# A diffusion block in fp32 on one core: the feed forwards as 2x2 block products with seven products for eight

## The chip, the cores and the metric

The kernel runs on one core of a Trainium2 chip. A core has five engines that work side by side, each through its own instructions in order: TensorE (PE; its weight loads are shown apart as PEld), VectorE (DVE), ScalarE (ACT), GpSimd (POOL) and SyncE (SP), which here starts nearly all DMAs. They share an SBUF of 128 partitions; matmuls are added up in PSUM. The metric is the time on the device of one execution, in microseconds (us), as the median of the runs.

## The reference

Two layers over 512 tokens `x` and 256 context tokens of 1024 values. Each layer is a feed forward, an attention (a grouped-query one with a window in layer 0, differential attention in layer 1) and a second feed forward; each is normed, scaled and shifted by a modulation, and its result is added to the residual:

```python
def _pre(h, gain, shift, scale):
    return _rmsnorm(h, gain) * (1.0 + scale) + shift

def _swiglu(h, w_gate, w_up, w_down):
    return (jax.nn.silu(h @ w_gate) * (h @ w_up)) @ w_down
...
        mx = (silu_c @ ada_w[i] + ada_b[i]).reshape(B, N_MOD, 1, D)
...
        fx = _swiglu(_pre(hx, norm_w[i, 0], mx[:, 0], mx[:, 1]), ffn_w_gate[i, 0], ffn_w_up[i, 0], ffn_w_down[i, 0])
        hx = hx + 0.5 * mx[:, 2] * fx
```

The context takes the same path with a modulation of its own; in the last feed forward (layer 1, the second) and in the final norm only `x` is left. Gate and up are 1024 x 2816, down 2816 x 1024; `ada_w` is 1024 x 9216 in each layer.

## The kernel before

All is held transposed: the residual `hT` is [128, 8, 768], eight blocks of 128 features for 768 tokens (256 of the context first). Every product takes three passes: each operand is split into a high part (rounded to float32r) and the rest, and high x high, high x low and low x high are added up in fp32 in PSUM. The gained residual stands split in `xh` and `xl`, with two more columns for the shift vectors. The norm's factor `rstd`, one per token, is applied after the product.

Weights are split when they are used. `weights` loads a packed 128 x 1024 unit (SP), casts it to the high part on ScalarE (L55) and subtracts that on GpSimd for the low part (L56); its pool holds two of each tile.

A block of gate or up (128 of 2816 columns, 22 blocks each) is `project`: 48 matmuls of 384 or 386 columns (L265) into two PSUM banks, then VectorE takes the bias columns (L270) and multiplies by `rstd` (L303). `up_block` runs it for gate and for up, then silu on ScalarE, (up + bias) x gate on VectorE (L952, the context's 256 columns and the 512 of `x`), the high part of the hidden block on ScalarE (L956) and its low part on GpSimd (L957).

Down follows in five groups of hidden blocks (`GROUPS`), each behind the first `up_block` of the next: for each of the eight output blocks a weight unit of 512 or 640 columns, `gemm` with the context's 256 and `x`'s 512 columns (L68, L70, L72), and `residual` on VectorE (L310). Behind the last group `after` makes squares and split parts of the block for what comes next. In the last feed forward all is done for the 512 columns of `x` alone (256 and 256), and `finish` takes the last group and the final norm, half of the tokens after the other.

The modulation is a matrix product with a vector, made on VectorE: `ada_block` loads 128 x 1024 of `ada_w` and multiplies with silu of the condition, with the sum as a second result (L130), once for `x` and, but for some of layer 1's, once for the context. The first 16 blocks come in `start` (twelve products there on GpSimd, L822), 56 in the first feed forward and 72 in the second, three and four behind each `up_block`.

The order on each engine is set when the program is built, by the framework's scheduler with its own model of times (`schedule_with_timeline_sim`); on the chip each queue runs in that order. L284, L491, L735 and others belong to the attentions.

## Time and profile before

| | |
|---|---|
| median of 3 runs | 2944.39 us (2941.35 to 2953.21) |
| profiled execution, first to last instruction | 2950.6 us |
| mean granted clock of TensorE | 0.977 |
| busy: PE, DVE, POOL, ACT | 95%, 53%, 44%, 33% |
| start and first feed forward | 0 to 656 us |
| window attention | to 1012 |
| second and third feed forward | to 1600 and 2155 |
| differential attention | to 2560 |
| last feed forward and final norm | to 2951 |

The profiled execution has no time but its span; it lies within the range of the timed runs. In rows that group instructions stand the line, the engine, the operation, what is written <- what is read by the program's names, the tile and how many; behind the bar the busy time, the mean of one in ns, and the engine's idle time ahead of them with what ended it. Rows by stretch give the busy time of each engine, the granted clock, the share of the DMA engines and GB/s. A timeline's row is start, duration, engine, line and operation.

### The profile page before, as it was taken

How to read it: one execution, taken by the hardware profiler on the slowest of the kernel's cores; microseconds unless marked ns; L12 is line 12 of the kernel's file. 1: busy time of each engine (PE TensorE's matmuls, PEld its weight loads, DVE VectorE, ACT ScalarE, POOL GpSimd, SP SyncE). 2: the span in 40 equal slices, each digit the busy share in tenths (PEclk: the TensorE clock that was granted, in tenths of full speed). 3: DMA queues.
4: the chain of work that ended last, by engine and by line, in shares of the span. 5: the costliest groups of instructions: out<-in, count | busy, mean ns of one | idle time of the engine just before them, and what ended most of it. 6: DMA issues, size and time to landing. Idle time of an engine off the chain costs nothing. (4 is left out here: it accounts for less than half of the span.)

```text
span 2950.6 us, 40979 instructions
## 1 busy us (share of the span) xinstructions
PE 2792.7 (95%) x16150; PEld 2608.6 (88%) x16150; DVE 1562.3 (53%) x2683; ACT 969.9 (33%) x1749; POOL 1303.5 (44%) x762
## 2 busy tenths in 40 slices
PE   5889999999989989999999999999999999999998
PEld 4878899999878888889999999999988888799998
DVE  7999422257787799632224322223267687522223
ACT  4211122144666421112223212122245565423223
POOL 5333333354543433333335333333365665656553
PEclk8999999999999999999999999999999999999999
DMA  6355212233342445631222121221122333233331
GB/s 236 123 175 201 86 58 72 65 102 102 84 140 76 139 158 192 236 94 54 68 65 65 59 63 58 71 63 50 61 85 79 88 88 105 93 93 102 101 100 64
DMA packets 113424, 296.38 MB, mean 100 GB/s; under 512 B 12880, under 2 KB 30928, under 8 KB 113232
## 3 DMA queue, kind: packets, MB, share of 16 engines
q1 hardware_dynamic: 112944, 293.66, 31.3%
q8 instruction: 128, 2.10, 0.3%
q14 instruction: 64, 0.52, 0.1%
q10 hardware_dynamic: 288, 0.10, 0.0%
HBM read 260.42 MB, written 15.20 MB: 93 GB/s over the span
## 5 line engine op out<-in xcount | busy, mean ns | idle before, releaser
L56 POOL TENSOR_TENSOR w_lo<-w_raw,w_hi 128x1024 fp32r<-128x1024 f32 (+2 forms) x377 | 793.2, 2105 | 1057.9 <-ACT w_hi L55 1037.0
L265 PE MATMUL big<-xh,w_hi 128*128 128x384 f32 (+3 forms) x2816 | 700.7, 330 | 44.0 <-DVE xh L830 16.3
L265 PE MATMUL big<-xh,w_lo 128*128 128x384 f32 (+3 forms) x2816 | 698.9, 330 | 21.4 <-POOL w_lo L56 21.4
L265 PE MATMUL big<-xl,w_hi 128*128 128x384 f32 (+3 forms) x2816 | 696.3, 328 | 4.3 <-DVE xl L831 4.3
L55 ACT CAST w_hi<-w_raw 128x1024 fp32r<-128x1024 f32 (+2 forms) x377 | 337.1, 894 | 1100.0 <-PE big L70 340.9
L265 PEld LDWEIGHTS big<-xh,w_hi 128*128 128x128 f32 x2816 | 505.4, 192 | 54.7 <-DVE xh L830 19.6
L265 PEld LDWEIGHTS big<-xh,w_lo 128*128 128x128 f32 x2816 | 501.8, 192 | 25.1 <-POOL w_lo L56 24.8
L265 PEld LDWEIGHTS big<-xl,w_hi 128*128 128x128 f32 x2816 | 504.0, 192 | 4.8 <-DVE xl L831 4.6
L270 DVE COPY bias<-big 128x2 f32<-128x2 f32 x176 | 27.7, 157 | 743.2 <-PE big L265 743.2
L130 DVE SCALAR_TENSOR_TENSOR ada_junk<-ada_raw,s_bc 128x1024 f32<-128x1024 f32 x224 | 339.7, 1549 | 44.8 <-DMA ada_raw<-ada_w 44.0
L310 DVE SCALAR_TENSOR_TENSOR hT<-big,mod,hT 128x512 f32<-128x512 f32 (+1 forms) x288 | 168.0, 619 | 352.7 <-PE big L72 352.6
L72 PE MATMUL big<-hh,w_lo 128*128 128x512 f32 (+1 forms) x1200 | 330.0, 347 | 7.7 <-POOL w_lo L56 7.7
L68 PE MATMUL big<-hh,w_hi 128*128 128x512 f32 (+1 forms) x1200 | 329.7, 346 | 0.7 <-ACT w_hi L55 0.7
L70 PE MATMUL big<-hl,w_hi 128*128 128x512 f32 (+1 forms) x1200 | 328.0, 344 | 0.0
L957 POOL TENSOR_TENSOR hl<-tb,hh 128x768 fp32r<-128x768 f32 (+1 forms) x88 | 153.1, 1740 | 262.5 <-ACT hh L956 239.7
L72 PEld LDWEIGHTS big<-hh,w_lo 128*128 128x128 f32 x1200 | 225.5, 189 | 38.5 <-POOL w_lo L56 10.0
L70 PEld LDWEIGHTS big<-hl,w_hi 128*128 128x128 f32 x1200 | 226.8, 189 | 30.6
L68 PEld LDWEIGHTS big<-hh,w_hi 128*128 128x128 f32 x1200 | 226.2, 189 | 29.5 <-ACT w_hi L55 1.4
L956 ACT CAST hh<-tb 128x768 fp32r<-128x768 f32 (+1 forms) x88 | 68.7, 781 | 347.6 <-DVE tb L952 347.6
L284 PE MATMUL half<-xh,w_hi 128*128 128x384 f32 (+3 forms) x464 | 156.1, 336 | 21.5 <-DVE ta L296 19.7
L952 DVE SCALAR_TENSOR_TENSOR tb<-tb,bias,ta 128x512 f32<-128x512 f32 (+1 forms) x154 | 169.2, 1132 | 6.8
L284 PE MATMUL half<-xl,w_hi 128*128 128x384 f32 (+3 forms) x464 | 154.2, 332 | 0.0
(215 smaller groups left out, 3689.8 us busy)
## 6 DMA issues: line engine op xcount, KB each, us to landing
w_raw<-ffn_gu SPq DMA_DIRECT2D x176, 512.0 KB, 3.3
ada_raw<-ada_w SPq DMA_DIRECT2D x144, 512.0 KB, 3.6
w_raw<-ffn_d SPq DMA_DIRECT2D x96, 256.0 KB, 2.7
w_raw<-ffn_d SPq DMA_DIRECT2D x64, 320.0 KB, 2.9
w_raw<-diff_in SPq DMA_DIRECT2D x24, 512.0 KB, 3.3
w_raw<-gqa_in SPq DMA_DIRECT2D x12, 512.0 KB, 3.4
og<-god SPq DMA_DIRECT2D x6, 768.0 KB, 5.9
w_raw<-gqa_out SPq DMA_DIRECT2D x8, 512.0 KB, 3.6
```

Of the source, the lines that this page charges most:

```text
L55: nc.scalar.copy(out=hi[:, :cols], in_=raw[:, :cols])
L56: nc.gpsimd.tensor_tensor(out=lo[:, :cols], in0=raw[:, :cols], in1=hi[:, :cols].bitcast(F32), op=ALU.subtract)
L68: nc.tensor.matmul(o, wh, xh, start=(k == 0), stop=False)
L70: nc.tensor.matmul(o, wh, xl, start=False, stop=False)
L72: nc.tensor.matmul(o, wl, xh, start=False, stop=(k == n - 1))
L130: getattr(nc, engines[s]).scalar_tensor_tensor(out=junk, in0=raw, scalar=1.0, in1=self.sbc[:, s], op0=ALU.mult, op1=ALU.mult, accum_out=se ...
L265: mm(ps[:, c, :e - s], w[:, k], x[:, k, s:e], start=first, stop=last)
L284: mm(ps[:, :e - s], w_[:, k], x[:, k, s:e], start=(k == 0 and i == 0), stop=(k == ND - 1 and i == 2))
L310: self.nc.vector.scalar_tensor_tensor(out=h, in0=o, scalar=self.mv(l, s, c, d), in1=h, op0=ALU.mult, op1=ALU.add)
L952: nc.vector.scalar_tensor_tensor(out=u[:, tk], in0=u[:, tk], scalar=bu[:, s:s + 1], in1=g[:, tk], op0=ALU.add, op1=ALU.mult)
L956: nc.scalar.copy(out=hh[:, toks], in_=u[:, toks])
L957: nc.gpsimd.tensor_tensor(out=hl[:, toks], in0=u[:, toks], in1=hh[:, toks].bitcast(F32), op=ALU.subtract)
```

## The change

The products of the feed forwards are written as 2x2 blocks. The left operand's four blocks are gate and up (or two output blocks of down) by the even and the odd 128-row blocks of the contracted side; the right operand's are the even and odd blocks by two halves of the tokens (384 and 384, in the last feed forward 256 and 256; the two bias columns go with the first half). Instead of eight block products there are seven of sums and differences (the Winograd form): `a_operands` loads four raw tiles of 512 columns for one block of gate and of up, makes four sums on VectorE (L116) and splits seven operands, the high parts on ScalarE and the low ones on GpSimd (L112). Raw tiles and sums come from one pool of eight buffers (`sf`), split operands from a ring of eight. `b_combine` makes the seven right operands (four differences on VectorE, L150; splits on GpSimd, L146 and L172, one on VectorE), once per feed forward for the input (`x_pair`) and once for the hidden blocks (`h_pair`).

The seven products go to three PSUM banks, with 84 matmuls for 96 per block of gate and up. The sums behind them are copies on ScalarE and additions from PSUM on VectorE (L1107, L1111, L1116, L1079); gate and the second half of up are multiplied by `rstd` on GpSimd (L1112, L1117). Product 4 of a block follows in the next. All blocks of gate and up come first; the hidden blocks are written to DRAM (`hs`) and read back in pairs for down, which has four groups (`PAIRS`, two pairs of hidden blocks and three times three) of four pairs of output blocks, with the additions straight into `hT` (L1139). In down an operand has 256 or 384 columns.

`next_pair` makes the next feed forward's operands behind each output pair; the squares' sums all move to VectorE (L245). The modulation blocks are spread over three feed forwards (48, 32, 48; L317), at most three behind a block of gate and up. In `start` only products 1, 5 and 2 of the first block are begun (before: three blocks). `finish` isn't split in halves. The attentions read the same split parts from other tiles, and their weights are split in tiles of 512.

```diff
-GROUPS = (5, 5, 4, 4, 4)
+KP = ND // 2
+PAIRS = (2, 3, 3, 3)
...
+    def sf_open(self, side="right"):
+        self.sf = self.sb("sums", 8, side=side)
...
+    PROD = {1: (0, 0), 2: (1, 1), 3: (6, 2), 4: (2, 6), 5: (4, 3), 6: (5, 4), 7: (3, 5)}
...
+    def a_operands(self, src, n):
...
+        def load(*bs):
+            for b in bs:
+                raws[b] = self.sf.tile([P, 512], F32, name="sf")[:, :n * P]
+                nc.sync.dma_start(raws[b], src[:, b])
+        def split(b, f):
+            ts[b] = self.wtile()
+            hi, lo = (ts[b][:, p, :n * P] for p in range(2))
+            nc.scalar.copy(out=hi, in_=f)
+            eng = nc.vector if b in self.dve_a else nc.gpsimd
+            eng.tensor_tensor(out=lo, in0=f, in1=hi.bitcast(F32), op=ALU.subtract)
...
+        def total(x, y, op=ALU.subtract):
+            t = self.sf.tile([P, 512], F32, name="sf")[:, :n * P]
+            nc.vector.tensor_tensor(out=t, in0=x, in1=y, op=op)
+            return t
...
+        load(0, 3, 2)
+        s1 = total(raw(3), raw(2), ALU.add)
+        s3 = total(raw(0), raw(3))
+        s2 = total(s1, raw(0))
+        split(0, raw(0))
+        split(4, s1)
+        load(1)
+        s4 = total(raw(1), s2)
+        split(1, raw(1))
+        split(5, s2)
+        split(6, s4)
+        split(3, s3)
+        split(2, raw(2))
...
+    def b_combine(self, t, w, f, splits):
...
+        t1 = diff(f(5), f(0))
+        if splits:
+            split(0, f(0))
+        split(3, t1)
+        if splits:
+            split(1, f(1))
+        t3 = diff(f(2), f(5))
+        t2 = diff(f(2), t1)
+        split(5, t3)
+        if splits:
+            split(2, f(2))
+        else:
+            raw = t[:, 0:3, 1, :w].bitcast(F32)
+            hi = t[:, 0:3, 0, :w]
+            nc.scalar.copy(out=hi, in_=raw)
+        t4 = diff(f(1), t2)
+        split(4, t2)
+        split(6, t4)
+        if not splits:
+            nc.gpsimd.tensor_tensor(out=t[:, 0:3, 1, :w], in0=raw, in1=hi.bitcast(F32), op=ALU.subtract)
+    def product(self, p, bank, aops, bops, w, ks=None, first=False):
...
+        wh, wl = aops[self.PROD[p][0]]
+        n = len(wh)
+        slot = self.PROD[p][1]
+        for k in (range(n) if ks is None else ks):
...
+            for x, y, go, end in ((wh[k], xh, first and k == 0, False), (wh[k], xl, False, False),
+                                  (wl[k], xh, False, k == n - 1)):
+                mm(bank[:, :w], x, y, start=go, stop=end, skip_group_check=not first)
...
+        parts = ((0, 2 * j, 0), (5, 2 * j, 1), (1, 2 * j + 1, 0), (2, 2 * j + 1, 1))
+        self.b_combine(t, B + m, source, True)
...
+    def squares(self, d, xonly=False):
...
+                sq = self.sf.tile([P, 512], F32, name="sf")[:, :m]
+                nc.scalar.activation(out=sq, in_=h[:, tk], func=AF.Square)
+                nc.vector.tensor_tensor(out=self.acc[:, tk], in0=sq, in1=self.acc[:, tk], op=ALU.add)
...
+    def next_pair(self, pools, l, n, j, xonly=False):
...
+        for d in (2 * j, 2 * j + 1):
+            self.squares(d, xonly)
+        t = self.optile(pools[0] if j < 3 else pools[1], xonly)
+        self.x_pair(t, l, n, j, xonly)
+        self.x.append(t)
...
+            if d % 2:
+                t = self.optile(pools[0] if d < 6 else pools[1], False)
+                self.x_pair(t, 0, 0, d // 2, False)
+                self.x.append(t)
+                self.up_begin(first, (d // 2,))
...
-        self.ffn(0, 0, False, [(0, b) for b in range(16, 72)], to_gqa, True)
...
-        self.ffn(0, 1, False, [(1, b) for b in range(72)],
-                 lambda d: (self.x_bias(1, 0) if d == 0 else None, self.x_block(1, 0, d)))
...
-        self.ffn(1, 0, False, [], lambda d: (self.x_bias(1, 1) if d == 0 else None, self.x_block(1, 1, d)))
...
+        self.ffn(0, 0, False, (self.opx, self.opy), [(0, b) for b in range(16, 64)], to_attention(0), True)
+        self.gqa()
+        pools = (self.opy, self.opx)
+        self.ffn(0, 1, False, pools, [(0, b) for b in range(64, 72)] + [(1, b) for b in range(24)],
+                 lambda j: self.next_pair(pools[::-1], 1, 0, j))
+        self.ffn(1, 0, False, pools[::-1], [(1, b) for b in range(24, 72)], to_attention(1))
...
+        self.ffn(1, 1, True, (self.opy, self.opx), [], lambda j: [self.squares(d, True) for d in (2 * j, 2 * j + 1)])
...
+        banks = [self.pbig.tile([P, 512], F32, name="bank") for _ in range(3)]
+        return (i, self.a_operands(self.a["ffn_gu"][l, f, i].rearrange("p (b n) -> p b n", b=4), KP), banks,
...
+    def up_begin(self, u, ks):
+        i, ops, (ba, bb, bc), w = u
+        for p, bank in ((1, ba), (5, bc), (2, bb)):
+            self.product(p, bank, ops, self.x, w, ks, True)
...
+        per = -(-len(todo) // (NFF - 4))
...
+        def up_end(i, ops, ba, g, u):
+            self.product(4, ba, ops, self.x, w)
+            nc.vector.tensor_tensor(out=u[:, B:w], in0=ba[:, B:w], in1=self.rstd[:, n1], op=ALU.mult)
+            ub = self.sp.tile([P, B], F32, name="bias")
+            nc.vector.tensor_copy(out=ub, in_=ba[:, 0:B])
...
+            for s, x, y in cuts:
+                nc.scalar.activation(out=g[:, x:y], in_=g[:, x:y], func=AF.Silu, bias=g[:, s:s + 1])
+            for s, x, y in cuts:
+                nc.vector.scalar_tensor_tensor(out=u[:, x:y], in0=u[:, x:y], scalar=ub[:, s:s + 1], in1=g[:, x:y],
                                                op0=ALU.add, op1=ALU.mult)
...
+            nc.sync.dma_start(hs[i][:, :2 * m], u[:, B:w + m])
...
+        for i in range(NFF):
...
+                unit = self.up_open(l, f, i, xonly)
...
+            if i:
+                prod(1, ba, True)
+            nc.scalar.copy(out=g[:, 0:w], in_=ba[:, :w])
+            if i:
+                prod(5, bc, True)
+            nc.scalar.copy(out=u[:, w:w + m], in_=bc[:, B:w])
+            if i:
+                prod(2, bb, True)
+            nc.vector.tensor_tensor(out=g[:, 0:w], in0=bb[:, :w], in1=g[:, 0:w], op=ALU.add)
+            prod(6, ba)
+            nc.scalar.copy(out=g[:, w:w + m], in_=ba[:, B:w])
+            prod(3, bc)
+            nc.vector.tensor_tensor(out=g[:, w:w + m], in0=bc[:, B:w], in1=g[:, w:w + m], op=ALU.add)
+            nc.gpsimd.tensor_tensor(out=g[:, B:w + m], in0=g[:, B:w + m], in1=self.rstd[:, t0:t0 + 2 * m], op=ALU.mult)
+            if late:
+                up_end(*late)
+            prod(7, ba)
+            nc.vector.tensor_tensor(out=u[:, w:w + m], in0=ba[:, B:w], in1=u[:, w:w + m], op=ALU.add)
+            nc.gpsimd.tensor_tensor(out=u[:, w:w + m], in0=u[:, w:w + m], in1=self.rstd[:, n2], op=ALU.mult)
+            late = (i, ops, ba, g, u)
...
+                    self.ada_block(*todo.pop(0))
+            if i >= NFF - 3 and len(h0) < 2:
+                h0.append(self.h_pair(pools[1], hs, len(h0), m, xonly))
+        up_end(*late)
...
+            for s, o, k in cuts:
+                h = self.hT[:, d, at + o:at + o + k]
+                nc.vector.scalar_tensor_tensor(out=h, in0=bank[:, o:o + k], scalar=self.mv(l, s, 2 if f == 0 else 8, d),
+                                               in1=h, op0=ALU.mult, op1=ALU.add)
...
+        def down_end(q, ops, bops, ba, last):
+            self.product(4, ba, ops, bops, m)
+            add(ba, 2 * q + 1, 0)
+            if last:
+                after(q)
...
+        for gi, n in enumerate(PAIRS):
...
+            for q in range(KP):
+                c = (off * KP + q * n) * 4 * P
+                ops = self.a_operands(a["ffn_d"][l, f, :, c:c + n * 4 * P].rearrange("p (b n) -> p b n", b=4), n)
+                ba, bb, bc = (self.pbig.tile([P, 512], F32, name="bank") for _ in range(3))
...
+                prod(1, ba, True)
+                add(ba, d1, 0)
+                prod(5, bc, True)
+                add(bc, d2, 1)
+                prod(2, bb, True)
+                add(bb, d1, 0)
+                prod(6, ba)
+                add(ba, d1, 1)
+                prod(3, bc)
+                add(bc, d1, 1)
+                if late:
+                    down_end(*late)
+                prod(7, ba)
+                add(ba, d2, 1)
+                late = (q, ops, hops, ba, last)
+                if not last and len(nxt) < PAIRS[gi + 1]:
+                    nxt.append(self.h_pair(pools[gi % 2], hs, off + n + len(nxt), m, xonly))
...
+    def h_pair(self, pool, hs, j, m, xonly):
+        t = self.optile(pool, xonly)
+        for slot, i, half in ((0, 0, 0), (5, 0, 1), (1, 1, 0), (2, 1, 1)):
+            self.nc.sync.dma_start(t[:, slot, 1, :m].bitcast(F32), hs[2 * j + i][:, half * m:half * m + m])
+        self.b_combine(t, m, lambda i: t[:, i, 1, :m].bitcast(F32), False)
```

Three places in the order. First GpSimd in gate/up; before, in the first feed forward (`w_lo` is the low part of the weights, `hl` that of a hidden block):

```order
L957 TENSOR_TENSOR hl<-tb,hh 128x768
L56 TENSOR_TENSOR w_lo<-w_raw,w_hi 128x1024 x2
L957 TENSOR_TENSOR hl<-tb,hh 128x768
L56 TENSOR_TENSOR w_lo<-w_raw,w_hi 128x1024 x2
L957 TENSOR_TENSOR hl<-tb,hh 128x768
```

and now, in one of the first three (`w` is a split operand, `ta` and `tb` gate and up):

```order
L112 TENSOR_TENSOR w<-sf,w 128x512 x5
L1112 TENSOR_TENSOR ta<-ta,rstd 128x768
L112 TENSOR_TENSOR w<-sf,w 128x512 x2
L1117 TENSOR_TENSOR tb<-tb,rstd 128x384
L112 TENSOR_TENSOR w<-sf,w 128x512 x5
```

One block of gate and up had two splits of 1024 and one of 768 columns; it has seven of 512 and the two products with `rstd`.

VectorE in gate/up with modulation; before, one block:

```order
L270 COPY bias<-big 128x2
L303 TENSOR_TENSOR ta<-big,rstd 128x768
L130 SCALAR_TENSOR_TENSOR ada_junk,mod<-ada_raw,s_bc 128x1024 x3
L270 COPY bias<-big 128x2
L303 TENSOR_TENSOR tb<-big,rstd 128x768
L130 SCALAR_TENSOR_TENSOR ada_junk,mod<-ada_raw,s_bc 128x1024 x2
L952 SCALAR_TENSOR_TENSOR tb<-tb,bias,ta 128x256
L952 SCALAR_TENSOR_TENSOR tb<-tb,bias,ta 128x512
```

and now (`op` is the tile that holds the modulation's input):

```order
L116 TENSOR_TENSOR sf<-sf 128x512
L317 SCALAR_TENSOR_TENSOR op,mod<-op 128x1024
L1111 TENSOR_TENSOR ta<-bank,ta 128x384
L116 TENSOR_TENSOR sf<-sf 128x512
L317 SCALAR_TENSOR_TENSOR op,mod<-op 128x1024
L1079 TENSOR_TENSOR tb<-bank,rstd 128x384
L1081 COPY bias<-bank 128x2
L116 TENSOR_TENSOR sf<-sf 128x512
L1116 TENSOR_TENSOR tb<-bank,tb 128x384
L317 SCALAR_TENSOR_TENSOR op,mod<-op 128x1024
L1086 SCALAR_TENSOR_TENSOR tb<-tb,bias,ta 128x256
L1086 SCALAR_TENSOR_TENSOR tb<-tb,bias,ta 128x512
```

The sums of the next block's operands (L116) stand between the modulation's products and the work that frees PSUM.

GpSimd in down; before, a group's eight weight units, with the next blocks of gate and up around them:

```order
L56 TENSOR_TENSOR w_lo<-w_raw,w_hi 128x640 x2
L957 TENSOR_TENSOR hl<-tb,hh 128x768
L56 TENSOR_TENSOR w_lo<-w_raw,w_hi 128x640 x6
L56 TENSOR_TENSOR w_lo<-w_raw,w_hi 128x1024 x4
L957 TENSOR_TENSOR hl<-tb,hh 128x768
```

and now, from the end of gate/up into the first group:

```order
L1117 TENSOR_TENSOR tb<-tb,rstd 128x384
L146 TENSOR_TENSOR op<-sf,op 128x384
L172 TENSOR_TENSOR op<-op 128x3x384
L146 TENSOR_TENSOR op<-sf,op 128x384 x2
L112 TENSOR_TENSOR w<-sf,w 128x256 x7
L172 TENSOR_TENSOR op<-op 128x3x384
```

The splits of the hidden pairs (L146, L172) stand between those of the weights (L112).

More of the change, by code (lines that the diff above doesn't have):

```diff
@@ L116, in ada_open @@
         nc, a = self.nc, self.a
-        self.sbc = pool.tile([P, 2, D], F32, name="s_bc")
+        t = self.optile(pool, False).rearrange("p a b n -> p (a b n)").bitcast(F32)
+        self.sbc = t[:, :2 * D].rearrange("p (s n) -> p s n", s=2)
+        self.ada_raw = [t[:, (2 + i) * D:(3 + i) * D] for i in range(2)]
+        self.ada_junk = t[:, 4 * D:5 * D]
+        self.ada_n = 0
         for s in range(2):
@@ L128, in ada_block @@
         for s in streams:
[L129 to L131 removed]
+            nc.vector.scalar_tensor_tensor(
+                out=self.ada_junk, in0=raw, scalar=1.0, in1=self.sbc[:, s], op0=ALU.mult, op1=ALU.mult,
                 accum_out=self.mod[:, l, s, b:b + 1])
@@ new lines, in norm_banks, with ffn @@
+    def norm_banks(self, xonly):
+        lo, m = (CTX, 256) if xonly else (0, 384)
+        ps = []
+        for i in range(2):
+            ps.append(self.pbig.tile([P, 512], F32, name="bank"))
+            self.nc.tensor.matmul(ps[i][:, :m], self.ones, self.acc[:, lo + i * m:lo + i * m + m], start=True,
+                                  stop=True)
+        self.bank_norm(ps, xonly)
+    def ffn(self, l, f, xonly, pools, side, after, first=False):
+        nc, a = self.nc, self.a
+        self.pbig = self.ps("pffn", 8)
+        self.w_open()
+        hs = self.dp.tile([NFF, P, T], F32, name=f"hs{l}{f}")
+        m = 256 if xonly else 384
+        w = B + m
+        t0 = CTX if xonly else 0
+        n1, n2 = slice(t0, t0 + m), slice(t0 + m, t0 + 2 * m)
@@ L927, in ffn @@
         todo = list(side)
-        per = -(-len(todo) // (NFF - 1))
+        per = -(-len(todo) // (NFF - 4))
         if first:
-            self.load_late()
-        else:
-            for which in range(2):
-                done[which, 0] = self.pbig.tile([P, 2, 512], F32, name="big")
-                self.project_k([(self.weights(a["ffn_gu"][l, f, which, 0]), done[which, 0])], range(ND), xonly)
-        self.norm(xonly, ssq)
-        if side and not first:
-            self.ada_open(self.adap)
@@ L939, in proj @@
[L939 to L958 removed]
+            self.ada_open(pools[1])
```

556 lines of the change are left out of this document (268 added, 288 removed).

## The prediction

> **What bounds the kernel now.** I read the page first, then the busy time by stage.
>
> ```profile
> span 2950.6 us, 40979 instructions
> PE 2792.7 (95%) x16150; PEld 2608.6 (88%) x16150; DVE 1562.3 (53%) x2683; ACT 969.9 (33%) x1749; POOL 1303.5 (44%) x762
> ```
>
> ```profile
> core 0: us, PE busy (x) PEld busy (x) DVE busy (x) ACT busy (x) POOL busy (x), PEclk, DMA share, GB/s
> 0.00:100.00 100.00, 60.21 (x224) 48.36 (x224) 80.88 (x116) 40.96 (x61) 48.16 (x23) 0.85 0.53 190
> 100.00:330.00 230.00, 209.92 (x1115) 200.15 (x1116) 214.12 (x316) 44.83 (x60) 85.77 (x37) 0.93 0.51 169
> 330.00:656.00 326.00, 326.00 (x1856) 308.67 (x1855) 100.19 (x144) 78.09 (x106) 127.28 (x71) 1.00 0.23 71
> 656.00:1012.00 356.00, 329.79 (x1898) 292.75 (x1897) 276.27 (x646) 214.05 (x536) 168.66 (x145) 0.98 0.35 106
> 1012.00:1290.00 278.00, 253.93 (x1356) 241.98 (x1355) 230.45 (x335) 55.11 (x70) 99.74 (x43) 0.94 0.55 183
> 1290.00:1600.00 310.00, 310.00 (x1763) 294.54 (x1762) 94.32 (x135) 73.80 (x101) 119.30 (x65) 1.00 0.20 62
> 1600.00:2155.00 555.00, 555.00 (x3152) 531.73 (x3151) 168.88 (x231) 132.90 (x176) 212.06 (x111) 1.00 0.20 62
> ...
> 2560.00:2951.00 391.00, 379.46 (x2738) 358.66 (x2736) 108.22 (x192) 117.53 (x165) 207.24 (x118) 0.99 0.29 91
> ```
>
> The rows are the start, the first feed forward with the modulation blocks (100 to 330) and without (to 656), the second (1012 to 1600), the third (1600 to 2155) and the last, on half of the columns (2560 on). Where no modulation runs, TensorE is busy in all of the time. Pieces of 25 us in the same columns show its pace:
>
> ```profile
> 50.00:75.00 25.00, 16.03 (x70) 14.64 (x69) 23.69 (x30) 9.53 (x16) 15.19 (x6) 0.75 0.33 101
> 300.00:325.00 25.00, 21.08 (x104) 20.44 (x103) 19.63 (x32) 6.52 (x9) 10.95 (x5) 0.86 0.36 117
> 475.00:500.00 25.00, 25.00 (x144) 25.00 (x143) 6.10 (x8) 6.24 (x8) 8.84 (x4) 1.00 0.19 64
> 2575.00:2600.00 25.00, 25.00 (x211) 25.00 (x210) 9.71 (x15) 7.86 (x10) 14.04 (x7) 1.00 0.29 89
> ```
>
> In gate/up 144 matmuls of 384 columns take 25 us, 0.174 us each; in the last feed forward 211 of 256 columns, 0.1185 us. So a unit (my word for one block of gate and of up, 96 matmuls) costs 16.7 and 11.4 us, and of the third's 555 us 22 units are 367 and down 188. Row 300:325, with modulation, has 104 matmuls at a clock of 0.86, and the waits of TensorE in 100:330 name what was late, the low part of the weights from POOL:
>
> ```profile
> PE big L265 <- POOL w_lo L56: 10.9, 4, 3.3
> PE big L265 <- ACT w_hi L55: 4.7, 3, 3.0
> ```
>
> So TensorE bounds the feed forwards, and where VectorE is full (214 of 230 us) POOL is already late at times. Prices come from the groups by shape in 375:600, where little disturbs them (busy us, then mean ns of one):
>
> ```profile
> L56 POOL TENSOR_TENSOR w_lo<-w_raw,w_hi 128x1024 fp32r<-128x1024 f32 x19 | 45.5, 2393 | 82.7 <-ACT w_hi L55 79.4 <-DMA w_raw<-ffn_gu 3.3
> L56 POOL TENSOR_TENSOR w_lo<-w_raw,w_hi 128x512 fp32r<-128x512 f32 x16 | 20.6, 1289 | 45.6 <-ACT w_hi L55 45.6
> L957 POOL TENSOR_TENSOR hl<-tb,hh 128x768 fp32r<-128x768 f32 x9 | 16.6, 1848 | 17.0 <-ACT hh L956 17.0
> ...
> L952 DVE SCALAR_TENSOR_TENSOR tb<-tb,bias,ta 128x512 f32<-128x512 f32 x9 | 6.7, 739 | 0.0
> L55 ACT CAST w_hi<-w_raw 128x512 fp32r<-128x512 f32 x16 | 9.9, 621 | 54.7 <-PE big L70 36.4 <-issue 12.0 <-PE big L265 6.3
> ```
>
> POOL takes 2.39, 1.29 and 1.85 us for 1024, 512 and 768 columns. From the whole run:
>
> ```profile
> L822 POOL TENSOR_TENSOR ada_junk<-ada_raw,s_bc 128x1024 f32<-128x1024 f32 x12 | 34.9, 2913 | 32.0 <-DVE ada_junk L825 19.7 <-issue 9.7 <-ACT xh L192 2.7
> L491 POOL TENSOR_TENSOR o<-o,oh 128x256 f32<-128x256 f32 x24 | 18.1, 755 | 38.3 <-ACT oh L490 26.0 <-PE half L284 6.3 <-issue 4.1
> ```
>
> 256 columns: 0.755 us. So 384 come to 1.02 (halfway to 512) and 1152 to 2.69 (0.56 per 256 more), both estimates. VectorE with both inputs in SBUF: 0.74 for 512 columns, and
>
> ```profile
> 170.10 1.14 DVE L952 SCALAR_TENSOR_TENSOR tb<-tb,bias,ta 128x256 f32<-128x256 f32 x2
> ```
>
> ```profile
> 2920.89 0.42 DVE L901 TENSOR_TENSOR acc<-ta,acc 128x256 f32<-128x256 f32 x1
> ```
>
> 1.14 for the pair of 256 and 512, 0.42 for 256, so 0.58 for 384. What decides is how the two engines stand to each other. VectorE, then POOL, in one stretch (start us, us):
>
> ```profile
> 150.52 1.22 DVE L130 SCALAR_TENSOR_TENSOR ada_junk<-ada_raw,s_bc 128x1024 f32<-128x1024 f32 x1
> ...
> 151.66 2.83 DVE L130 SCALAR_TENSOR_TENSOR ada_junk<-ada_raw,s_bc 128x1024 f32<-128x1024 f32 x1
> ...
> 154.50 0.94 DVE L303 TENSOR_TENSOR ta<-big,rstd 128x768 f32<-128x768 f32 x1
> 155.37 2.42 DVE L130 SCALAR_TENSOR_TENSOR ada_junk<-ada_raw,s_bc 128x1024 f32<-128x1024 f32 x1
> ```
>
> ```profile
> 151.55 1.87 POOL L957 TENSOR_TENSOR hl<-tb,hh 128x768 fp32r<-128x768 f32 x1 [10.04 <-ACT hh L956]
> 153.38 3.33 POOL L56 TENSOR_TENSOR w_lo<-w_raw,w_hi 128x1024 fp32r<-128x1024 f32 x1
> 157.62 2.40 POOL L56 TENSOR_TENSOR w_lo<-w_raw,w_hi 128x1024 fp32r<-128x1024 f32 x1 [0.92 <-ACT w_hi L55]
> ```
>
> A modulation product of 1024 columns takes 1.22 us alone. The one that starts at 151.66 runs into POOL's instruction, which ends at 153.42, and ends at 154.50, 1.08 us later. POOL's next began at 153.38 and ends at 156.70, 2.20 us after that product instead of 2.39. The third product waits again, to 157.79. But L303, which reads PSUM, takes its usual 0.94 at 154.50 inside POOL's instruction. So a POOL instruction and a VectorE one with two SBUF inputs do not run side by side: their times add. I call that the shared door.
>
> **The change, part by part.** TensorE: a unit falls from 96 to 84 matmuls, 84 x 0.1736 = 14.6 us (last feed forward: 9.95); down from 188 us to 924 matmuls of 384 columns, 160 us (last: 924 x 0.1185 = 109). Three full feed forwards at 22 x 14.6 + 160 = 481 and the last at 328 are 1771 us of TensorE; they now last 556 + 588 + 555 + 391 = 2090 by the stage rows. Were TensorE all, 319 us would be gained.
>
> The door, per unit. Before: two POOL splits of 1024 and one of 768 (6.6) and the pair L952 (1.14), 7.8 us, plus 7.3 with three modulation blocks of two products of 1.22: 15.1, under TensorE's 16.7. After: seven splits of 512 (9.03), gate times rstd (1.85), up times rstd (1.02), so POOL alone has 11.9; VectorE's four sums of 512 (2.96) and the pair (1.14): **16.0 us**, over TensorE's 14.6. The copies and sums out of PSUM stay outside, like L303. A modulation block adds 2.44 us (two products) or 1.22 (one). That the mean is 1.55 is the door's price already:
>
> ```profile
> L130 DVE SCALAR_TENSOR_TENSOR ada_junk<-ada_raw,s_bc 128x1024 f32<-128x1024 f32 x224 | 339.7, 1549 | 44.8 <-DMA ada_raw<-ada_w 44.0
> ```
>
> They are spread anew: 48 blocks in the first feed forward, 32 in the second, 48 in the third (16 with two products, 32 with one). At three, two and three of them in a unit, gate/up is, first: 16 x 23.3 + 6 x 16.0 = 469; second: 16 x 20.9 + 96 = 430; third: 22 x 16.0 + 16 x 2.44 + 32 x 1.22 = 430. Each also reads back two pairs of hidden blocks: three POOL splits of 384 columns and one of 1152 (5.75), five VectorE instructions of 384 (2.9), 8.65 a pair, so 17 us. The last feed forward: POOL 9.03 + 1.29 + 0.755, VectorE 5 x 0.74, 14.8 us a unit, 325 in all (TensorE 219), and two hidden pairs of 6.2 (POOL 3 x 0.755 + 1.85, VectorE 5 x 0.42).
>
> Down, per pair of output blocks: seven splits and four sums, 7.0 us in the first group (256 columns) and 9.5 in the others (384); TensorE 7.3 and 10.9. Each group but the last also makes three hidden pairs of 8.65. So its four output pairs come to 54, 64 and 64 us; the last to 38 and what follows it: squares and parts of eight blocks for the attention (2 x 0.58 + 1.14 each), 18, or, where the next feed forward's operands are made, four times six splits and nine VectorE instructions (11.3), 45. That is 238, 265 and 238 us. Last feed forward: 47 + 57 + 57 + 45 = 205.
>
> Sums at the door: first 469 + 17 + 238 - 12 (unit 0 is split in the start) = 712; second 712; third 685; last 542; together **2651 us**, against TensorE's 1771. Not each duration counts in full: behind another, a product of 1.22 holds the door 1.08, a split of 2.39 holds it 2.20, about 0.9 of the sum; and in the fullest stretch now (214 of 230 us) 7% stays empty. 0.89 / 0.93 = 0.95, which I take: 2518. Bounds: 0.87 with nothing empty, 2306; above, full durations and 5% empty, 2790.
>
> Outside: in the start POOL has 12 products (34.9 us busy, L822), 24 splits of 384 and 7 of 512, VectorE 20 modulation products, 20 sums of 384 and 4 of 512: 68 + 39 = 107 us against 100 now, about +15 with the units that TensorE no longer begins there. Behind the first attention the fourth operand pair (11.3) is made after the output projection, +15; behind the second +8; the end loses the split in two halves of the tokens, +8. These four are estimates, 46 us, bounds 0 and 100. Moving the hidden blocks through DRAM is 8.7 MB each way per feed forward against a DMA share of 0.20 to 0.55: nothing, hidden by the 15 us and more that a unit takes; without that cover one landing:
>
> ```profile
> w_raw<-ffn_d SPq DMA_DIRECT2D x96, 256.0 KB, 2.7
> ```
>
> Forecast: 2950.6 - 2090 + 2518 + 46 = 3425 us for the profiled span. The runs have a median 6 us below that span, so **3420**.
>
> TensorE will now have gaps. Row 50:75, where it is busy in 16 of 25 us, grants it 0.75 of its clock; rival (3) uses that. The Trainium skill ("TensorE: Matmul & The Clock Gate", Part 1) says that an idle window of about 3.4 us halves the clock: kept down throughout, TensorE's 1771 us would be 3542 and the time about 4450. No row here grants so little, so it gets no chance of its own.
>
> **Rivals.** (1) The door is no limit because the splits find TensorE's slack; POOL alone then counts: units at 14.6 (last: 11.1 x 22 = 244), groups of 38 to 53: 507 + 515 + 507 + 396 = 1925, so 2950.6 - 2090 + 1925 + 30 = 2816 us, faster. For it: before ran door and TensorE side by side; against it: three waits in the stretch above. If POOL were hidden as well, 1771 gives 2660. (2) The order: raw tiles and sums share eight buffers, just one unit's, so the next unit's third raw tile loads only when the last split of this one is done. From there 2.7 (landing) + 0.74 (sum) + 0.62 (the cast L55) pass until POOL has its second split, and it has 2.3 us of other work: 1.8 us idle in each of 88 units and 64 output pairs, 274 us more, 3700. For it: every engine keeps its order; against it: the door's other user fills such gaps. (3) The granted clock falls to 0.75 throughout. TensorE needs 2361, still under the door's 2518; but units without modulation rise from 15.2 to 14.6 / 0.75 = 19.5 (18 of them, 77 us) and three last groups by 5: 3515. For it: row 50:75; against it: row 656:1012, with as many short gaps in the attention, at 0.98. That the change would not cut the matmuls is no rival: the counts are in the code.
>
> **How the numbers follow.** Door as summed 0.73, (1) 0.07 and 2660 another 0.02, (2) 0.12, (3) 0.06. The range 3210 to 3660 holds the bounds of the sum (2306 gives 3213), (3) and the nearer part of (2). A measurement here tells apart some 0.5%. Faster 0.09, the same 0.02, slower 0.89.
>
> **What would show it.** Right: TensorE busy near 70% of the span, POOL near 70% or more; units with three modulation blocks 21 to 24 us apart, without any 15 to 17, in the last feed forward 14 to 15; the sums of 512 columns on VectorE well over 0.74 us in the mean, the splits over 1.29, while evacuations from PSUM keep their time; TensorE's waits led by the low parts from POOL. Wrong: units at 14.6 us, or VectorE sums at 0.74 inside POOL instructions; for (2), waits of VectorE's sums for DMA; for (3), slices at clock 0.8 where nothing else is late.

## The result and the profile after

The changed kernel takes 3396.9 us in the median (3396.0 to 3406.3), the one before 2944.8: a ratio of 1.154, with an interval of 1.151 to 1.156. The forecast was 3420 us, within 3210 to 3660. The profiled execution is 3395.8 us. Its page, the span and the engines:

```profile
span 3395.8 us, 45475 instructions
PE 2748.3 (81%) x14996; PEld 2556.0 (75%) x14996; DVE 2625.6 (77%) x4098; ACT 1450.1 (43%) x3070; POOL 2500.7 (74%) x1894
```

The trace has 1154 matmuls fewer, and GpSimd's busy time has nearly doubled (it was 1303.5 us). By stage, in the columns shown of before (start and first unit; gate/up of the first feed forward; its down; window attention; gate/up and down of the second and of the third; differential attention; gate/up of the last; its down and the final norm):

```profile
0.00:122.00 122.00, 39.28 (x92) 23.89 (x92) 110.61 (x146) 51.00 (x95) 82.62 (x57) 0.61 0.42 149
122.00:543.00 421.00, 352.00 (x1789) 342.32 (x1790) 368.54 (x438) 143.53 (x271) 344.57 (x206) 0.91 0.41 127
543.00:772.00 229.00, 186.06 (x924) 168.78 (x923) 182.49 (x308) 90.26 (x180) 168.90 (x143) 0.93 0.29 94
772.00:1166.00 394.00, 327.90 (x1856) 290.00 (x1856) 281.93 (x684) 223.82 (x581) 183.42 (x188) 0.93 0.32 95
1166.00:1588.00 422.00, 358.51 (x1852) 347.23 (x1853) 335.70 (x404) 155.89 (x288) 335.96 (x213) 0.92 0.37 115
1588.00:1838.00 250.00, 188.33 (x927) 175.09 (x926) 203.39 (x329) 104.82 (x208) 200.75 (x175) 0.90 0.27 86
1838.00:2257.00 419.00, 360.30 (x1854) 348.25 (x1853) 332.89 (x400) 155.85 (x288) 336.45 (x213) 0.93 0.43 137
2257.00:2482.00 225.00, 181.54 (x925) 164.63 (x924) 184.29 (x317) 91.45 (x184) 171.67 (x144) 0.95 0.28 88
2482.00:2894.00 412.00, 358.69 (x2006) 320.43 (x2006) 275.74 (x590) 225.75 (x546) 243.97 (x207) 0.96 0.30 87
2894.00:3197.00 303.00, 252.68 (x1852) 242.52 (x1852) 197.18 (x239) 131.56 (x262) 284.01 (x212) 0.93 0.32 98
3197.00:3396.00 199.00, 143.05 (x930) 132.81 (x928) 152.82 (x250) 76.18 (x171) 148.35 (x144) 0.83 0.30 92
```

| stage | before | forecast | measured |
|---|---|---|---|
| start and first feed forward | 656 | 100 + 15 + 0.95 x 712 = 791 | 772 |
| window attention | 356 | 371 | 394 |
| second feed forward | 588 | 676 | 672 |
| third | 555 | 651 | 644 |
| differential attention | 405 | 413 | 412 |
| last, with the norm | 391 | 0.95 x 542 + 8 = 523 | 502 |
| sum | 2951 | 3425 | 3396 |

Of the 445 us lost 400 lie in the feed forwards, and every stage is within 23 us of its forecast. The groups by shape show how; busy us, then the mean of one in ns:

```profile
L112 POOL TENSOR_TENSOR w<-sf,w 128x512 fp32r<-128x512 f32 x616 | 1005.9, 1656 | 87.8 <-ACT w L110 85.0 <-PE bank L185 1.1 <-POOL w L112 1.1
L116 DVE TENSOR_TENSOR sf<-sf 128x512 f32<-128x512 f32 x352 | 424.3, 1215 | 211.4 <-DMA sf<-ffn_gu 191.7 <-POOL w L112 18.4
L317 DVE SCALAR_TENSOR_TENSOR op<-op 128x1024 f32<-128x1024 f32 x224 | 405.2, 1809 | 15.6 <-DMA op<-ada_w 14.0
...
L1111 DVE TENSOR_TENSOR ta<-bank,ta 128x384 f32<-128x384 f32 x66 | 36.2, 549 | 5.4 <-PE bank L185 4.5 <-ACT ta L1109 0.7
```

The sums of 512 columns with both inputs in SBUF take 1.215 us instead of some 0.74, the splits 1.656 instead of 1.289, the modulation products 1.809 instead of 1.22 alone. L1111, which reads PSUM, has 0.549 us for 384 columns, where L303 took 0.94 for 768 before. In one stretch of a unit with modulation, VectorE and then GpSimd (start, duration):

```profile
1229.09 1.34 DVE L116 TENSOR_TENSOR sf<-sf 128x512 f32<-128x512 f32 x1
1230.36 2.30 DVE L317 SCALAR_TENSOR_TENSOR op<-op 128x1024 f32<-128x1024 f32 x1
...
1232.59 0.55 DVE L1107 TENSOR_TENSOR ta<-bank,ta 128x386 f32<-128x386 f32 x1
1233.06 1.82 DVE L317 SCALAR_TENSOR_TENSOR op<-op 128x1024 f32<-128x1024 f32 x1
```

```profile
1229.84 6.19 POOL L112 TENSOR_TENSOR w<-sf,w 128x512 fp32r<-128x512 f32 x3
```

The product at 1230.36 starts half a microsecond after GpSimd's three splits and ends 2.3 us later; the one from PSUM at 1232.59 takes its 0.55 inside the same splits; GpSimd's three take 6.19 us instead of 3.87.

Counted from the single instructions (the union of all of GpSimd's with VectorE's lines that read two SBUF operands), this shared door was in use in 94% of the second feed forward's stretch with modulation (1204 to 1407), 92% of the rest of its gate/up, 97% of the last gate/up and 84 to 87% of the downs. Before it was 88% and 80% in the two stretches with modulation and 43% in the rest of the first three feed forwards. TensorE waits, by what came last:

```profile
PE bank L185 <- ACT w L110: 115.9, 69, 10.8
PE bank L185 <- DVE tb L1116: 115.1, 43, 8.1
PE bank L185 <- DVE hT L1139: 93.0, 76, 3.5
PE bank L185 <- ACT op L144: 55.7, 21, 10.6
PE bank L185 <- ACT ta L1101: 38.9, 20, 7.0
PE bank L185 <- POOL w L112: 38.4, 26, 5.0
```

Only the sixth row is GpSimd itself. The casts (L110) and the additions behind products (L1116, L1139) are work for which ScalarE or VectorE came late, and the casts themselves waited most for VectorE's sums (L116):

```profile
L110 ACT CAST w<-sf 128x512 fp32r<-128x512 f32 (+2 forms) x1064 | 571.6, 563 | 700.3 <-DVE sf L116 343.0
```

The order is not quite the one that the sum assumed. The products of the modulation lie mostly in the first twelve, eight and ten units after unit 0, with three to nine in a unit (single instructions counted); the sum had them in sixteen units each, with three to six. The scheduler made them earlier than they are written. The sum over a feed forward does not change by that.

### The profile page after: what moved, and what is told of

Same layout as the page of the kernel before. It is cut to its first block, busy times and chain, and to the rows that moved or that the text cites. A ratio compares the mean times of both kernels' runs of the same rounds, so it can differ in the third digit from the quotient of the medians.

```text
span 3395.8 us, 45475 instructions
## 1 busy us (share of the span) xinstructions
PE 2748.3 (81%) x14996; PEld 2556.0 (75%) x14996; DVE 2625.6 (77%) x4098; ACT 1450.1 (43%) x3070; POOL 2500.7 (74%) x1894
## 5 line engine op out<-in xcount | busy, mean ns | idle before, releaser
L185 PE MATMUL bank<-op,w 128*128 128x386 f32 (+3 forms) x11088 | 2041.4, 345 | 496.6 <-ACT w L110 115.9
L185 PEld LDWEIGHTS bank<-op,w 128*128 128x128 f32 x11088 | 1934.5, 203 | 605.6 <-ACT w L110 145.8
L112 POOL TENSOR_TENSOR w<-sf,w 128x512 fp32r<-128x512 f32 (+2 forms) x1064 | 1492.8, 1429 | 178.1 <-ACT w L110 174.4
L116 DVE TENSOR_TENSOR sf<-sf 128x512 f32<-128x512 f32 (+2 forms) x608 | 667.2, 1113 | 275.2 <-DMA sf<-ffn_gu 191.7
L110 ACT CAST w<-sf 128x512 fp32r<-128x512 f32 (+2 forms) x1064 | 571.6, 563 | 700.3 <-DVE sf L116 343.0
L317 DVE SCALAR_TENSOR_TENSOR op<-op 128x1024 f32<-128x1024 f32 x224 | 405.2, 1809 | 15.6 <-DMA op<-ada_w 14.0
L146 POOL TENSOR_TENSOR op<-sf,op 128x384 fp32r<-128x384 f32 (+3 forms) x228 | 264.7, 1177 | 144.5 <-ACT op L144 144.4
L1139 DVE SCALAR_TENSOR_TENSOR hT<-bank,mod,hT 128x256 f32<-128x256 f32 (+1 forms) x592 | 271.3, 486 | 93.2 <-PE bank L185 90.7
L414 PE MATMUL half<-op,w 128*128 128x384 f32 (+3 forms) x1392 | 254.6, 331 | 15.2 <-DVE ta L426 14.6
L414 PEld LDWEIGHTS half<-op,w 128*128 128x128 f32 x1392 | 228.7, 190 | 26.6 <-DVE ta L426 14.8
L1112 POOL TENSOR_TENSOR ta<-ta,rstd 128x768 f32<-128x768 f32 (+1 forms) x88 | 155.4, 1766 | 121.3 <-DVE ta L1111 112.9
L1117 POOL TENSOR_TENSOR tb<-tb,rstd 128x384 f32<-128x384 f32 (+1 forms) x88 | 98.5, 1119 | 58.6 <-DVE tb L1116 57.1
L646 PE MATMUL half<-og,w 128*128 128x256 f32 (+1 forms) x384 | 77.6, 356 | 27.7 <-ACT w L83 26.9
L150 DVE TENSOR_TENSOR sf<-op 128x384 f32<-128x384 f32 (+1 forms) x88 | 82.5, 963 | 16.3 <-DMA op<-hs 14.2
L172 POOL TENSOR_TENSOR op<-op 128x1152 fp32r<-128x1152 f32 (+1 forms) x44 | 92.0, 2090 | 1.6 <-DVE sf L150 1.1
```

The costliest lines, as they stand in the source:

```text
L110: nc.scalar.copy(out=hi, in_=f)
L112: eng.tensor_tensor(out=lo, in0=f, in1=hi.bitcast(F32), op=ALU.subtract)
L116: nc.vector.tensor_tensor(out=t, in0=x, in1=y, op=op)
L146: eng.tensor_tensor(out=lo, in0=x, in1=hi.bitcast(F32), op=ALU.subtract)
L185: mm(bank[:, :w], x, y, start=go, stop=end, skip_group_check=not first)
L317: nc.vector.scalar_tensor_tensor(out=self.ada_junk, in0=raw, scalar=1.0, in1=self.sbc[:, s], op0=ALU.mult, op1=ALU.mult, accum_out=self.mo ...
```

## Experiments

**Splits on VectorE.** If the two engines exclude each other, work is cheaper on the faster one, even if that is the fuller one.

```diff
-    dve_a = ()
+    dve_a = tuple(range(7))
```

> The seven low parts of the weights' operands are subtracted on VectorE instead of GpSimd; everything else stays. Shared door (a GpSimd instruction and a VectorE one with two SBUF inputs exclude each other): a split of 512 columns holds the door 0.74 us instead of 1.29, so a unit falls from 16.0 to 2.9 + 4.1 + 7 x 0.74 = 12.2 us, under TensorE's 14.6; with three two-product modulation blocks 19.5 instead of 23.3. Over the four feed forwards the door sum falls by some 450 us: about 2950 us (2870 to 3050). If the two engines work side by side and each is limited by its own load, VectorE, at 77% of the span, gets some 650 us more: 3450 or more. If the wait is for raw tiles and the order of the queues: about 3400, no change.

Measured: 3145.6 us, 1.069 (1.067 to 1.071) of before and 251 us less than the change. The engine that already had more work got 760 us of splits more (486 in the shape shown) and the whole became faster: that decides against engines limited each by its own load. VectorE's busy time rose by only 95 us (2625.6 to 2721.0), for its other instructions became shorter. From its groups:

```profile
L112 DVE TENSOR_TENSOR w<-sf,w 128x512 fp32r<-128x512 f32 x616 | 485.7, 803 | 5.7 <-ACT w L110 5.6
L317 DVE SCALAR_TENSOR_TENSOR op<-op 128x1024 f32<-128x1024 f32 x224 | 298.5, 1333 | 1.9 <-DMA op<-ada_w 1.3
L116 DVE TENSOR_TENSOR sf<-sf 128x512 f32<-128x512 f32 x352 | 273.7, 788 | 48.0 <-DMA sf<-ffn_gu 46.1 <-DVE w L112 0.9 <-DVE bias L1081 0.6
```

The sums are at 0.788 us, the products of the modulation at 1.333. Units (starts of their products on TensorE) are now mostly 14.9 us apart, with modulation 15 to 17, where they were 20 to 24. Some 200 us of the expected 450 did not come. Near half of that is missing in down: 221, 234, 220 and 163 us instead of the 191, 218, 191 and 150 that the door's sum gives. There VectorE itself is full, 200 of the 222 us in the third feed forward's down:

```profile
2068.00:2290.00 222.00, 186.29 (x940) 171.09 (x938) 200.39 (x423) 88.59 (x182) 56.04 (x38) 0.94 0.29 92
```

My door sum leaves VectorE's ten additions from PSUM per pair of output blocks out, rightly; but when the splits move to VectorE they queue behind them. The other half is in gate/up, where the expectation let a unit fall with the door's sum to 12.2 us; it stops at TensorE's 14.9, and the first feed forward's last unit but one took 48 us, with 16 products of the modulation in it. The scheduler also spread the products over 20, 15 and 15 units here, so part of the gain with modulation may be the spread; how much was not tested. The last feed forward has no modulation: its gate/up fell from 306 to 263 us (first to last matmul).

**The modulation: less work, or the same work off the door.** In one kernel the products have 8 columns, and the rest of the sum is left out; in the other 1024, with the second input in a PSUM bank.

```diff
-                out=self.ada_junk, in0=raw, scalar=1.0, in1=self.sbc[:, s], ...
+                out=self.ada_junk[:, :8], in0=raw[:, :8], scalar=1.0, in1=self.sbc[:, s, :8], ...
```

> The modulation's products behind the blocks of gate and up read 8 columns instead of 1024 (the rest of the sum is left out); loads and instruction counts stay. Shared door: units with modulation, 20 to 22 us apart now, fall to the 15 to 16 us of those without: 16 x 6 + 16 x 5 + 16 x 5 = 256 us less, about 3140 us. Engines limited by their own load: with three blocks VectorE has 7.3 + 4.1 + 2.2 = 13.6 us per unit, under TensorE's 14.6, so taking 7.3 away gives little: 3350 to 3400.

```diff
+        self.mc = self.pmod.tile([P, 1, 512], F32, name="mc")
+        nc.scalar.copy(out=self.mc[:, 0], in_=self.sbc[:, 0, :512])
...
-                out=self.ada_junk, in0=raw, scalar=1.0, in1=self.sbc[:, s], ...
+                out=self.ada_junk.rearrange("p (c n) -> p c n", c=2), in0=raw.rearrange("p (c n) -> p c n", c=2),
+                scalar=1.0, in1=self.mc.to_broadcast([P, 2, 512]), ...
...
```

> The modulation's products stay 1024 columns long and as many, but their second input is read from PSUM: one bank that holds the first 512 values of the condition of x, read twice (so the result leaves out the other half and the context's condition); the products' ring has seven banks for eight. Shared door: an instruction with one input from PSUM does not hold it, so the time falls nearly as with the 8 columns although VectorE does the same work: 3140 to 3200 us, the product's mean falls from 1.81 to 1.2 us. If VectorE's own load counts, or memory traffic in general: 3400, the mean stays.

Measured (one run each): 3277.4 and 3265.5 us, 120 and 131 less than the change. The group of the 8 columns, and that of the products with an input in PSUM:

```profile
L317 DVE SCALAR_TENSOR_TENSOR op<-op 128x8 f32<-128x8 f32 x224 | 127.4, 569 | 102.4 <-DMA op<-ada_w 98.4 <-ACT op L307 1.3
```

```profile
L319 DVE SCALAR_TENSOR_TENSOR op<-op,mc 128x1024 f32<-128x1024 f32 x224 | 271.5, 1212 | 40.1 <-DMA op<-ada_w 34.7 <-ACT mc L309 4.0
```

This is the cleanest answer. The full 1024 columns take 1.212 us when one input comes from PSUM, against 1.809 from SBUF in the same place, and the time falls as much as if the work were left out. Of the 224 products 193 ran beside a GpSimd instruction, and each took 1.20 to 1.22 us. And 8 columns still take 0.569 us in the mean: not work, but the wait for the splits in front. The 102 that met no GpSimd instruction took 0.16 us, the 122 that overlapped one 0.91, and every one over 0.3 us ended within 0.25 us of the end of a GpSimd instruction. What counts here is not VectorE's load but its use of the door. The Trainium skill ("SBUF — State Buffer", "SBUF: two separate sides") states it so: a port pair shared by VectorE and GpSimd, held exclusively for a whole instruction, on VectorE's side by one with two SBUF inputs. These rows agree.

The size was half of the expected 256 us in both. With 8 columns gate/up fell from 412, 384 and 381 us (units 1 to 21 of the first three feed forwards) to 365, 352 and 350; units with modulation are still 16 to 24 us apart. With the door freer, loads came last: with 8 columns DMA was busy in 68% of 122 to 250 us,

```profile
122.00:250.00 128.00, 109.85 (x545) 105.91 (x543) 94.58 (x222) 44.25 (x81) 85.28 (x62) 0.89 0.68 223
```

and over the run VectorE's sums wait 263 us for raw tiles of gate and up and its products 98 us for their own (the change: 192 and 14). Part of that is the order: the scheduler packed the 8-column products, with their loads of 512 KB, into the first seven, four and seven units after unit 0. With the input in PSUM they lie in twelve, eight and nine, as in the change, so that kernel is the closer comparison; its sums wait 211 us and its products 35.

**GpSimd's splits of the weights left out.** Each low part becomes a second copy of the raw value on ScalarE.

```diff
-            eng.tensor_tensor(out=lo, in0=f, in1=hi.bitcast(F32), op=ALU.subtract)
+            nc.scalar.copy(out=lo, in_=f)
```

> The low part of each weight operand is a second copy of the raw value on ScalarE instead of GpSimd's subtraction (the subtraction is left out, so the third pass is wrong). Shared door: GpSimd loses 1493 us of instructions; a unit's door falls to 7.0 us (14.3 with modulation), ScalarE has about 14 us of work per unit, so TensorE's 14.6 us bound: 2700 to 2850 us, VectorE's sums at their free 0.74 us. If the eight buffers and the landing of raw tiles bound the units, they stay above 15 us: 3100 or more.

Measured (one run): 2980.3 us, 417 less than the change, but 130 to 280 more than expected. Gate/up did as expected: nearly all units without modulation are 14.9 us apart, in the last feed forward 10.1, and the sums are near the 0.74 us that they take alone:

```profile
L116 DVE TENSOR_TENSOR sf<-sf 128x512 f32<-128x512 f32 x352 | 266.8, 769 | 190.8 <-DMA sf<-ffn_gu 163.8 <-ACT w L112 22.2 <-POOL ta L1112 2.2
```

The rest is in what I had put at nothing or too low: down 193, 209, 191 and 145 us against TensorE's 160 and 109; the first unit of the second and the third feed forward at 35 to 37 us, from its first matmul to the next unit's, instead of 15; the window attention at 394. What sets the pace there was not tested. So even without these splits on GpSimd seven products would not have beaten the kernel before in this shape.

**The ring of raw tiles** (second rival). One buffer more, once on the kernel with 8 columns and once on the change itself.

```diff
-        self.sf = self.sb("sums", 8, side=side)
+        self.sf = self.sb("sums", 9, side=side)
```

> Modulation products of 8 columns as in the earlier run, and nine buffers instead of eight for raw tiles and sums, so that the next block's third raw tile no longer waits for the last split of this one. With 8 columns the units with modulation stayed near 18 us, and raw tiles waited 142 us for splits on GpSimd between 110 and 450 us. If that ring is what bounds the units once the door is freed: they fall to 15 to 16 us, 3277 - 16 x 2 x 3 = 3180 us (3150 to 3220). If it is the order of the loads behind the modulation's own: no change, 3260 to 3280.

> The changed kernel with nine buffers for raw tiles and sums, nothing else. Shared door as the bound: GpSimd or a VectorE instruction of this kind is already busy in 89 to 96% of gate/up, so little can be won: 3340 to 3390 us. If the raw tiles' wait for the ring is the bound (the second rival of the prediction): 1.8 us in each of 88 units and 64 output pairs, 3130 to 3200.

Measured: 3246.2 us (one run), 31 less than with 8 columns and eight buffers and between the two times expected; and 3396.2 us for the change with nine, no difference. The second rival falls as a cause of the time. But the traces show a share of it: with nine buffers most units without modulation are 14.9 us apart in both kernels, where they were 15 to 17, 16 in the mean. In the change this took a few us from the first gate/up and some 13 from each of the next two; the last lost 4, and the downs, first units and attentions took the rest back. With 8 columns and nine buffers the last feed forward's units are very evenly 12.6 us apart, but for the last three, and the door is in use in 99% of that time (2745 to 3000 us): 0.85 of the 14.8 us of my sum.

**Down with eight products.** On top of the splits on VectorE, down is made from the same tiles without sums, with splits on GpSimd; a pair of output blocks has four operands and six additions.

```diff
-                ops = self.a_operands(a["ffn_d"][l, f, :, c:c + n * 4 * P].rearrange("p (b n) -> p b n", b=4), n)
+                ops = self.a_plain(a["ffn_d"][l, f, :, c:c + n * 4 * P].rearrange("p (b n) -> p b n", b=4), n)
...
+                                for half in range(2):
+                                    mm(banks[half][:, :m], w_, b[:, k * 2 + half, part, :m], start=go, stop=end)
+                    for half in range(2):
+                        add(banks[half], 2 * q + d, half)
```

> On top of the splits on VectorE, down is made with the plain eight block products from the same tiles (four splits on GpSimd per pair of output blocks, no sums, six additions into the residual instead of ten; the hidden pairs need four splits and no differences); gate/up keeps the seven products. TensorE then needs 4 x 8.3 + 12 x 12.5 = 183 us for a down (125 in the last feed forward) instead of 160 (109). If it is the work on VectorE and GpSimd that sets the pace of down (220, 233, 220 and 163 us there with the splits on VectorE, VectorE busy in 92% of a piece), down falls to about 193, 205, 193 and 135: 3145 - 112 = 3035 us (2990 to 3080). If TensorE sets it, down rises by a seventh: 3250.

Measured: 3062.7 us, 1.038 (1.036 to 1.041) of before; 83 us less than with seven products. A pair takes 8.4 and 12.6 us, TensorE's own time, in the first three groups but for their first pair; only the last group is slower (14 to 24 us), where `after` makes the next operands. With a seventh more matmuls down is faster. This kernel also has down's splits on GpSimd again; so has the change itself, whose four downs take 906 us from their first matmul to their last, against 795 here. The sums, differences, three more splits and extra additions cost more than they save.

**The kernel before, its modulation spread.** If the door bounds the stretches with modulation there too, spreading its blocks as the change does should win time without any block products.

```diff
-            for _ in range(per):
-                if todo:
-                    self.ada_block(self.adap, *todo.pop(0))
+            while todo and (len(side) - len(todo)) * (NFF - 1) < (i + 1) * len(side):
+                self.ada_block(self.adap, *todo.pop(0))
...
-        self.ffn(0, 0, False, [(0, b) for b in range(16, 72)], to_gqa, True)
+        self.ffn(0, 0, False, [(0, b) for b in range(16, 64)], to_gqa, True)
...
```

> The kernel before, with nothing changed but the place of the modulation blocks: 48, 32 and 48 in the first three feed forwards, spread evenly over their 21 blocks of gate and up. Shared door: 2.3 blocks of two products per block of gate and up put 7.8 + 5.6 = 13.4 us on the door, under TensorE's 16.7, so the 36 and 42 us that TensorE loses in the two stretches with modulation vanish: about 2875 us (2855 to 2900). If those losses come from loads or from the clock and not from the door, they move with the blocks: 2930 to 2950.

Measured: 2947.3 us, 0.999 (0.998 to 1.000), no difference. The expectation failed because the edit did not do what it says: the scheduler pulled the products forward, and all 224 were still made before 300 us and between 950 and 1300. So it told nothing of the door; the next one pins them.

```diff
-            getattr(nc, engines[s]).scalar_tensor_tensor(
+            self.tc.keep_in_program_order(getattr(nc, engines[s]).scalar_tensor_tensor(
```

> As the run before it with the kernel before (48, 32 and 48 modulation blocks), but each product is pinned behind what stands ahead of it on VectorE, so the scheduler can't pull it forward: in that run all 224 products still lay between 50 and 300 and between 950 and 1300 us, as densely as in the kernel before. Shared door: 13.4 us per block of gate and up, under TensorE's 16.7, so the blocks with modulation, 20 to 23 us apart, fall to 17 and most of the 36 and 42 us come back: 2880 us (2860 to 2910). If the losses come from loads or the clock: 2935 to 2950.

Measured: 2875.1 us, 0.976 (0.975 to 0.978) of before. The same two stretches, and the groups:

```profile
100.00:330.00 230.00, 230.00 (x1311) 220.17 (x1310) 159.29 (x203) 49.11 (x64) 97.57 (x44) 1.00 0.36 122
...
1000.00:1290.00 290.00, 290.00 (x1650) 279.61 (x1649) 146.55 (x190) 61.53 (x78) 113.44 (x54) 1.00 0.30 99
```

```profile
L56 POOL TENSOR_TENSOR w_lo<-w_raw,w_hi 128x1024 fp32r<-128x1024 f32 x225 | 573.8, 2550 | 720.4 <-ACT w_hi L55 710.9 <-DMA w_raw<-ffn_gu 6.7 <-ACT p L449 2.7
L130 DVE SCALAR_TENSOR_TENSOR ada_junk<-ada_raw,s_bc 128x1024 f32<-128x1024 f32 x224 | 404.6, 1850 | 3.7 <-DMA ada_raw<-ada_w 3.7
```

TensorE is busy in all of 100 to 330 us (210 before), and of 1000 to 1290, at a clock of 1.00. The products take longer than before (1.850 us, 1.549 there) and GpSimd's splits a little (2.550, 2.505): the waits at the door are still there, but wholly behind TensorE. That the door was what the 70 us were lost to is not shown by this: the spread also thins VectorE's own work (214 to 159 us of the 230) and the loads (DMA share 0.51 to 0.36) in the same stretch.

```diff
-                    if c == 0 and (s == 1 or d % 2 == 1):
+                    if False:
```

> In addition the start's twelve products on GpSimd (2.9 us each, with sums on ScalarE) go to VectorE (1.22 each). Shared door: the start's door falls from 59 us of products to 39, so the first 105 us shorten by 10 to 20: 2865 us. If VectorE's own load counts there (81 of 100 us busy): 15 us more than without this edit.

Measured: 2860.3 us, 0.971 (0.969 to 0.973) of before, the fastest version found. The first 100 us, in the run before it and with this edit:

```profile
0.00:100.00 100.00, 61.33 (x235) 50.09 (x236) 76.30 (x110) 43.89 (x65) 48.13 (x24) 0.83 0.48 180
```

```profile
0.00:100.00 100.00, 72.07 (x324) 60.18 (x325) 84.29 (x150) 34.81 (x45) 23.99 (x15) 0.95 0.53 198
```

The first hidden block's split starts at 88 us instead of 104; VectorE's 12 products more cost less than GpSimd's 12 did.

## Why the prediction was right, point by point

- **The shared door as the mechanism**: right, and now shown: by the sums at 1.215 us beside L1111's 0.549, by the products of 1024 columns that an input in PSUM brings from 1.809 to 1.212, by the 8-column products at 0.16 us alone and 0.91 beside GpSimd, and by 251 us won by loading the fuller engine.
- **TensorE's term**: a unit at 14.6 us is 14.9 where nothing disturbs it; the count of 84 matmuls is right.
- **Two signs that did not come**: TensorE was to be busy near 70% of the span, and was in 81%; its waits were to be led by the low parts from GpSimd, and these came sixth, with 38.4 us. The door made VectorE late more than GpSimd: the largest wait, for ScalarE's casts, goes back to VectorE's sums, and the second and third are VectorE's own additions. The door's sum holds whichever of the two comes late, but the path to TensorE was another than the one named.
- **Units with modulation, 21 to 24 us**: measured mostly 20 to 24, 18 to 26 at the ends, in fewer and fuller units than the sum had. Their price was called all door; the two runs with the modulation off the door show 120 to 131 us for it, and behind that the loads, which had no term of their own. Here the sum was right with one cause too few. How much of the rest is SP's order and how much the DMA engines stays open.
- **Units without modulation, "15 to 17"**: measured so, 16 in the mean, but the door alone did not set that: with one buffer more, with or without short modulation products, they are at TensorE's 14.9 with the door in use in 96 to 98%. The two limits nearly coincide there, and the second rival's ring added the rest. The last feed forward's units were forecast 14 to 15 us apart and are 10 to 18, 12.8 in the mean but for the last three.
- **The factor 0.95**: too high for the door alone: 0.97 of 14.9 us in use are 0.90 of my 16.0, and the last feed forward shows 0.85 of the summed durations (12.6 of 14.8 us, with nine buffers and the door in use in 99%); my lower bound was 0.87. Its 7% left empty was VectorE's busy share (214 of 230 us), not the door's, which was in use in 88% there. 0.95 held the total because it covered other waits, and that is luck in part. The range did not hold all that it says: the upper bound of the sum, 2790, gives 3697 us, above 3660.
- **Down at 226, 252, 226 us**: measured 229, 250 and 225, by luck in part: the door was in use in only 84 to 87% of them. VectorE's additions from PSUM are outside the door but in VectorE's own queue, and TensorE waits 93 us for them (L1139). The plain down shows that both together cost more than a seventh more matmuls.
- **Extras of 46 us**: the window attention cost 38 more, not 15; TensorE waits 26.9 us there for two casts of the output projection's weights (L646), which it did not before. The differential attention's 8 and the end were right.
- **Rivals.** (1), GpSimd as the only limit, at 2816 us, falls: GpSimd had the same 1894 instructions where the PSUM input won 131 us. (2) falls as the bound, with the share just told. (3): the clock is 0.91 in the mean, 0.61 only in the start; TensorE was not what set the pace, and with the splits on VectorE its mean rose to 0.937 by itself. The Trainium skill's half clock after idle windows ("TensorE: Matmul & The Clock Gate", Part 1) gave an estimate of 4450 us if it were kept down throughout. The trace does not show that: no stage but the start is under 0.83.

## What to carry over

Two engines that shut each other out are one resource: add up the times of the instructions that use it, from both, and compare that sum with the bound engine's time per unit; off-loading from the faster to the slower of the two then makes the sum larger, even where the faster one is the fuller. A saving in matmuls is paid in sums, splits and additions on the engines behind TensorE, so count these per unit before; here an eighth of the matmuls was worth 1.8 us a unit, and the added work more. And where a scheduler sets the order, look in the new order whether a moved instruction has moved, and whether others moved with it: spreading the modulation in the code did nothing until it was pinned, and then won 2.4%, and two of the experiments above changed the modulation's order though no line of their edits moves it.

## What was not expected

An instruction of 8 columns that takes 0.16 us alone costs 0.91 if it meets the other engine's instruction at the door: short instructions do not slip through. And with the door in use in 88% of a stretch the kernel before lost 36 us of TensorE in 230 (1115 matmuls at 0.1736 us are 194), while at 13.4 us of summed durations per block, with the door in use in 66%, it lost nothing at all; VectorE's own load and the loads fell with it, so the door's part of that stays open.
